# ConvFFN of a two-layer trunk: rstd moved from the FFN's input to its outputs, and the second group of columns computed in Strassen's block products

## The chip, the cores and the metric

One core of a Trainium2 chip runs the whole program. The metric is the device time of one execution in microseconds (us). TensorE is called PE here, VectorE DVE, ScalarE ACT, GpSimd POOL, and SyncE's DMA queue SP. PEld is PE's weight load, which runs beside its matmuls.

## The reference

The program computes a decoder trunk of two layers for 512 tokens of width 1024, in float32. Each layer is a pre-norm mixer and a pre-norm gated ConvFFN with residuals. What bears on this change:

```
def rms_norm(x, g):
    y = x32 * lax.rsqrt(jnp.mean(x32 * x32, axis=-1, keepdims=True) + EPS)
    return y.astype(x.dtype) * g

def gated_conv_ffn(x, w_gate, w_up, conv_w, conv_b, w_down):
    g = jnp.einsum('bsd,df->bsf', x, w_gate)
    g = causal_dwconv3(g, conv_w) + conv_b
    up = jnp.einsum('bsd,df->bsf', x, w_up)
    return jnp.einsum('bsf,fd->bsd', jax.nn.silu(g) * up, w_down)

h = h + gated_conv_ffn(rms_norm(h, norm_ffn[layer]), ...)
```

D_FF is 2816, that is 22 tiles of 128 columns. The factor rsqrt(mean) (called rstd, or r) belongs to a token, so it commutes with every product over the width: it may stand on the input of the two up-projections or on their outputs. The gate needs it ahead of its convolution over tokens; the up branch enters linearly, so its factor may stand anywhere up to the output of the down-projection.

## The kernel before

**Layout.** h is held as 8 tiles of 128 channels x 512 tokens. Every float32 operand of a matmul is split into two parts, hi (rounded by ACT) and lo (the rest, by DVE's subtraction or, in `summed`, L136, by an ACT copy of -x to which a DMA issued on POOL adds x). A product of two such operands is three matmuls (`mm3`, L152): hi·hi, hi·lo, lo·hi.

**The FFN.** It works through gate and up columns in groups of two tiles each (f, f+1), f = 0, 2, ..., 20, and after every second group adds the down-projection of the last four tiles to the residual (`PARTS`, L516; the first part projects two tiles only, so groups 0 and 2 run ahead of it). Layer 0 projects onto h with channels on the partitions (`project`, L286), layer 1 onto y with tokens on the partitions (`down` and `done`, L1106 and L1145).

- Group 0 (`direct`, L592) multiplies in the plain way: 4 column tiles x 8 channel tiles x 3 matmuls, each of 512 tokens. Its input is not normalized yet: hg holds gain·h. The norm's sums of squares are finished beside it, `rstd_cols` and `rstd_spread` (L222, L212) make r, and `evacuate` (L607) multiplies the gate by r on DVE (L615) and, after silu, the product's other factor by r on POOL (L618).
- Meanwhile `normalize` (L626) forms h·gain·r for all 8 channel tiles on DVE, splits it anew into hg (which group 0 is still reading), and makes the block sums t23 and t41 that Strassen's products need, split into halves too: by DVE for the first two pairs of channel tiles, by POOL's DMAs for the other two.
- Group 2 also runs `direct`, on the normalized hg, two column tiles at a time.
- Groups 4 to 20 run `both` (L681), Strassen's seven block products for gate and for up: 14 products of 4 x 3 matmuls, each of 256 tokens. The weights are first combined on DVE (s12, s34: L698 to L707) and split; `after` (L727) gathers products from PSUM into a padded row (gate) or into `kept` (up). After the products "g 4" and "g 3" the gate rows go through the convolution (`conv`, L561: one ACT scaling, two DVE operations) and silu. L750 to L755 multiply by the up part and split the result into the activations a_hi (ACT) and a_lo (DVE, L262).

**What sets the order.** The code is written in the order of priority, but each engine's queue is laid down ahead of time by the framework's planner, which takes the first instruction in this order whose inputs and buffers it reckons to be ready. So a matmul of a later product can be put ahead of one that would have to wait. On the chip each queue then runs in its fixed order. `inorder` pins single instructions to the written order, `behind` (L84) puts one behind another. Buffers bound it further: 7 PSUM banks for products, 6 weight units (whi, wlo), 4 activations, 3 tiles of the tag "sum" (x, t, s12, s34), 3 padded rows. The input weights arrive on SP's queue, whatever POOL adds to arrives on POOL's.

Of the kernel before, what the change touches and what calls it, by code (L numbers as in the profile page):

```python
# [32 lines left out]
def tile_trunk(ctx: ExitStack, tc: tile.TileContext, x, norm_mix, norm_ffn, final_norm,  # L33
# [102 lines left out]
    def summed(raw, a, b, name):  # L136

        hi = wp.tile([P, a, b], F32R, tag="whi", bufs=6, name=f"whi_{name}")
        lo = wp.tile([P, a, b], F32R, tag="wlo", bufs=6, name=f"wlo_{name}")
        first = nc.scalar.activation(lo, raw, AF.Copy, scale=-1.0)  # L140
        nc.gpsimd.dma_start(lo, raw, accum_op=ALU.add)  # L141
        behind(nc.scalar.activation(hi, raw, AF.Copy), first)
        return hi, lo
# [42 lines left out]
    def hg_k(k):  # L186
        return hg[k][0], hg[k][1]
# [358 lines left out]
    class Ffn:  # L546
# [7 lines left out]

        def __init__(self, layer, prm, norm, ap, sums):
# [3 lines left out]
            self.added = {"g": None, "u": None}  # L559

# [17 lines left out]
        def pair_weights(self, f, order, by_dma=""):  # L578

            ch = {}  # L580
            for key, half in order:
                name = f"{key}{self.layer}_{f}_{half}"
                raw = wp.tile([P, 4, 2 * P], F32, tag="raw", bufs=4, name=f"raw_{name}")
                w = (w_ffn_gate if key == "g" else w_ffn_up)[self.layer][:, f * P : (f + 2) * P]
# [4 lines left out]
                ch[key, half] = (summed if key in by_dma else parts)(raw, 4, 2 * P, name)  # L589
            return ch  # L590

        def direct(self, f, normed, sets, ch, before=lambda i, j: None):  # L592
# [3 lines left out]
            for js in sets:  # L596
                for i, k in enumerate(PAIRS):
                    for j in js:
                        before(i, j)
                        hi, lo = ch["gu"[j // 2], i // 4]  # L600
                        c = slice((j % 2) * P, (j % 2 + 1) * P)
                        if j not in banks:
                            banks[j] = mm_bank(f"gu{layer}_{f}_{j}")
                        mm3(banks[j], (hi[:, i % 4, c], lo[:, i % 4, c]), hg_k(k),
                            i == 0, i == NK - 1)

            def evacuate():  # L607
                r = self.r
                gates = []
                for j in range(2):  # L610
                    t = padded_tile()
                    if normed:
                        nc.scalar.copy(t[:, 2:], banks[j])
                    else:
                        nc.vector.tensor_tensor(t[:, 2:], banks[j], r, ALU.mult)  # L615
                    s = self.silu(self.conv(t, f + j), f + j)
                    if not normed:
                        nc.gpsimd.tensor_tensor(s, s, r, ALU.mult)  # L618
                    gates.append(s)
                for j, s in enumerate(gates):  # L620
                    nc.vector.tensor_tensor(s, banks[2 + j], s, ALU.mult)
                    self.act(f + j, s)
# [3 lines left out]
        def normalize(self, kp):  # L626

            n, r = f"{self.layer}_{kp}", self.r
            x = self.ap.tile([P, 2, S], F32, tag="sum", bufs=3, name=f"x{n}")
            for i, k in enumerate((kp, kp + NP)):  # L630
                nc.vector.scalar_tensor_tensor(x[:, i, :], h[k], self.prm("ffn", k), r,
                                               op0=ALU.mult, op1=ALU.mult)

            def halves(dst, src):
                nc.scalar.activation(dst[0], src, AF.Copy)
                nc.vector.tensor_tensor(dst[1], src, dst[0].bitcast(F32), ALU.subtract)

            halves(hg[kp], x[:, 0, :])
            halves(hg[kp + NP], x[:, 1, :])
            b11, b12 = x[:, 0, :HALF], x[:, 0, HALF:]  # L640
            b21, b22 = x[:, 1, :HALF], x[:, 1, HALF:]
# [546 lines left out]
```

## Time and profile before

| what | value |
|---|---|
| median of 3 runs | 994.29 us (994.14 to 994.36) |
| the profiled execution's own time | 994.15 us |
| its span, first to last instruction | 992.4 us |
| DVE busy | 728.5 us (73%) |
| ACT busy | 536.3 us (54%) |
| POOL busy | 105.3 us (11%) |
| bytes moved by DMA | 125.07 MB, mean 126 GB/s |

The profile is of one execution. A line of the timeline gives start, duration, engine, the code's line, the operation, output <- inputs, partitions x elements, and in brackets the idle time of that engine just before it with what ended it. A line of the windows gives, for a stretch from:to in us, its length and each engine's busy time with the number of instructions. A line of the groups gives the number of instructions after x, then busy time in all and the mean duration in ns. DVE's and ACT's durations overlap by some hundredths at their ends, so what an instruction costs its engine is the distance from one start to the next. The span is 1.75 us shorter than the execution's own time.

### The profile page before, as it was taken

To read this page: it belongs to the slowest core of one execution; us is meant where nothing else is said; L and a number is where in the kernel's file an instruction comes from. 1 tells how busy PE (TensorE), PEld (TensorE's weight loads), DVE (VectorE), ACT (ScalarE), POOL (GpSimd) and SP (SyncE) were. 2 spreads that over 40 slices of the span, in tenths; PEclk is the share of its full clock that TensorE was granted. 3 is DMA by queue.
4 is the path that set the end of the run, shared out by engine and by line. 5 is a ranking of instruction groups with operands and counts; after the bars stand their busy time and mean duration, and the time that the engine had idled before them with its cause. 6 is when DMAs were issued, how large, how long until landed. Compare 5 with 4: busy or idle time off the path is not lost.

```text
span 992.4 us, 14934 instructions
## 1 busy us (share of the span) xinstructions
PE 982.9 (99%) x5905; PEld 875.6 (88%) x5905; DVE 728.5 (73%) x1104; ACT 536.3 (54%) x806; POOL 105.3 (11%) x121
## 2 busy tenths in 40 slices
PE   9999999999999999999999999999999999999997
PEld 6788888898999989999888988888989899898996
DVE  6897458967785877858988665399668768687676
ACT  5623346744653746537668634675546366363664
POOL 2141031200000000000300001211000010000100
PEclk9999999999999999999999999999999999999999
DMA  7442225544553645536423513435546456464542
GB/s 246 133 146 85 86 88 131 121 148 118 133 147 97 181 121 132 148 98 180 136 87 93 182 54 97 105 91 130 143 101 159 124 125 173 94 163 126 123 112 85
DMA packets 83073, 125.07 MB, mean 126 GB/s; under 512 B 4308, under 2 KB 56252, under 8 KB 83004
## 3 DMA queue, kind: packets, MB, share of 16 engines
q1 hardware_dynamic: 74028, 98.24, 31.4%
q0 software_dynamic: 7056, 23.60, 13.3%
q10 hardware_dynamic: 1920, 2.30, 0.7%
q8 instruction: 46, 0.75, 0.3%
q14 instruction: 23, 0.19, 0.1%
HBM read 98.42 MB, written 2.10 MB: 101 GB/s over the span
## 4 chain that ended last, share of the span: by engine, by line
PE 94%; issue 1%; DVE 1%; DMA 1%; ACT 0%; DVEq 0%; POOLq 0%; ACTq 0%
PE d L154 4%; PE d L153 4%; PE d L155 4%; PE dn L153 4%; PE dn L154 4%; PE dn L155 4%; PE gu L153 3%; PE gu L154 3%; PE gu L155 3%; PE v L153 1%; PE oo L155 1%; PE oo L153 1%; PE v L155 1%; PE oe L155 1%; PE oe L154 1%; PE v L154 1%
## 5 line engine op out<-in xcount | busy, mean ns | idle before, releaser
L153 PE MATMUL dn<-whi_dn,a_hi 128*128 128x512 f32 (+1 forms) x180 | 69.4, 386 | 0.0
L154 PE MATMUL dn<-wlo_dn,a_hi 128*128 128x512 f32 (+1 forms) x180 | 69.3, 385 | 0.0
L154 PE MATMUL d<-a_lo,whi_d 128*128 128x512 f32 x176 | 68.7, 390 | 0.0
L155 PE MATMUL d<-a_hi,wlo_d 128*128 128x512 f32 x176 | 68.5, 389 | 0.0
L155 PE MATMUL dn<-whi_dn,a_lo 128*128 128x512 f32 (+1 forms) x180 | 67.9, 385 | 0.0
L153 PE MATMUL d<-a_hi,whi_d 128*128 128x512 f32 x176 | 66.9, 390 | 0.0
L566 DVE SCALAR_TENSOR_TENSOR c<-rows,prm,c 128x512 f32<-128x512 f32 x88 | 66.4, 766 | 0.0
L141 POOL DMA_DIRECT2D wlo_g<-raw_g x22 | 19.1, 867 | 373.9 <-ACT wlo_g L140 257.9
L1109 DVE TENSOR_TENSOR y<-dn,y 128x512 f32<-128x512 f32 (+1 forms) x49 | 32.5, 674 | 23.3 <-PE dn L155 23.0
L140 ACT ACTIVATE wlo_g<-raw_g 128x1024 fp32r<-128x1024 f32 x22 | 23.2, 1056 | 42.4 <-PE dn L154 42.4
L572 ACT ACTIVATE s<-c,prm 128x512 f32<-128x512 f32 x44 | 31.7, 720 | 20.5 <-DVE c L566 20.4
L679 DVE TENSOR_TENSOR wlo_s34u<-s34u,whi_s34u 128x1024 fp32r<-128x1024 f32 x18 | 22.0, 1225 | 27.9 <-ACT whi_s34u L678 27.9
L155 PEld LDWEIGHTS dn<-whi_dn,a_lo 128*128 128x128 f32 x180 | 33.8, 188 | 7.3 <-DVE a_lo L262 0.2
L678 ACT ACTIVATE whi_s12u<-s12u 128x1024 fp32r<-128x1024 f32 x18 | 18.9, 1051 | 39.3 <-PE d L154 33.7
L153 PEld LDWEIGHTS dn<-whi_dn,a_hi 128*128 128x128 f32 x180 | 33.8, 188 | 7.0 <-ACT a_hi L260 0.2
L154 PEld LDWEIGHTS dn<-wlo_dn,a_hi 128*128 128x128 f32 x180 | 33.8, 188 | 6.4
L154 PEld LDWEIGHTS d<-a_lo,whi_d 128*128 128x128 f32 x176 | 33.1, 188 | 7.3 <-DVE a_lo L262 0.2
L305 DVE TENSOR_TENSOR h<-d,h 128x512 f32<-128x512 f32 x48 | 32.5, 683 | 9.2 <-PE d L155 9.2
L153 PEld LDWEIGHTS d<-a_hi,whi_d 128*128 128x128 f32 x176 | 32.8, 188 | 7.0
L155 PEld LDWEIGHTS d<-a_hi,wlo_d 128*128 128x128 f32 x176 | 33.0, 188 | 6.7
L260 ACT ACTIVATE a_hi<-s 128x512 fp32r<-128x512 f32 x44 | 27.6, 628 | 16.1 <-DVE s L751 7.4
L149 DVE TENSOR_TENSOR wlo_dn<-raw_dn,whi_dn 128x1024 fp32r<-128x1024 f32 x22 | 26.8, 1220 | 11.6 <-ACT whi_dn L148 11.6
(1274 smaller groups left out, 3469.1 us busy)
## 6 DMA issues: line engine op xcount, KB each, us to landing
raw_g<-in_w_ffn_gate_dram SPq DMA_DIRECT2D x36, 512.0 KB, 4.6
raw_u<-in_w_ffn_up_dram SPq DMA_DIRECT2D x36, 512.0 KB, 4.7
wlo_g<-raw_g POOLq DMA_DIRECT2D x22, 512.0 KB, 4.7
raw_d<-in_w_ffn_down_dram SPq DMA_DIRECT2D x22, 512.0 KB, 4.0
raw_dn<-in_w_ffn_down_dram SPq DMA_DIRECT2D x22, 512.0 KB, 4.0
wlo_u<-raw_u POOLq DMA_DIRECT2D x19, 512.0 KB, 4.6
raw_oe<-in_w_out_even_dram SPq DMA_DIRECT2D x8, 512.0 KB, 3.6
raw_g<-in_w_ffn_gate_dram SPq DMA_DIRECT2D x16, 256.0 KB, 2.9
```

The source lines that it names most:

```text
L140: first = nc.scalar.activation(lo, raw, AF.Copy, scale=-1.0)
L141: nc.gpsimd.dma_start(lo, raw, accum_op=ALU.add)
L149: behind(nc.vector.tensor_tensor(lo, raw, hi.bitcast(F32), ALU.subtract), after[0])
L153: nc.tensor.matmul(ps, lhs[0], rhs[0], start=start, stop=False)
L154: nc.tensor.matmul(ps, lhs[0], rhs[1], start=False, stop=False)
L155: nc.tensor.matmul(ps, lhs[1], rhs[0], start=False, stop=stop)
L260: nc.scalar.activation(hi, src, AF.Copy, scale=scale)
L305: nc.vector.tensor_tensor(h[k], ps, h[k], ALU.add)
L566: nc.vector.scalar_tensor_tensor(c, t[:, i : S + i], prm("cf", i * NF + ft), c, op0=ALU.mult, op1=ALU.add)
L572: nc.scalar.activation(s, c, AF.Silu, bias=self.prm("bf", ft))
L679: nc.vector.tensor_tensor(lo, src, hi.bitcast(F32), ALU.subtract)
L1109: nc.vector.tensor_tensor(dst, ps, dst, ALU.add)
```

## The change

hg stays gain·h for the whole FFN, and r is applied behind the products. Group 2 runs `both` like the groups after it, and `direct` is left to group 0. In detail:

- `normalize` becomes `block_sums`: ACT scales one channel tile of a pair by the gain into the sum tile, DVE forms the four block sums from it and from h, and the sums are split as before, t41 ahead of t23. hg is not rewritten, and r is not needed for it.
- In `both`, each gate row is multiplied by r on DVE ahead of the convolution. In layer 0, whose down-projection has tokens along the free axis, DVE also multiplies the up branch's part by r: s[1] after its silu, and the first two blocks of kept. In layer 1 the factor of the up branch is applied where the down-projection's result is added to y: a column per token tile, as the scalar of one DVE operation in place of the plain addition. For that the column form of r is kept in `cols`.
- In `direct`, the multiplication by r after silu moves from POOL to DVE in layer 0 and goes away in layer 1.
- `summed` gets a hook: in `both` the split of s12 is written between the ACT copy that precedes POOL's DMA and the ACT copy of hi, where it stood ahead of both.

```
-    def summed(raw, a, b, name):
+    def summed(raw, a, b, name, between=lambda: None):
...
         first = nc.scalar.activation(lo, raw, AF.Copy, scale=-1.0)
         nc.gpsimd.dma_start(lo, raw, accum_op=ALU.add)
+        between()
         behind(nc.scalar.activation(hi, raw, AF.Copy), first)
...
+            self.cols = small[:, 3 * PAD : 3 * PAD + NT]
...
-                    if normed:
-                        nc.scalar.copy(t[:, 2:], banks[j])
-                    else:
-                        nc.vector.tensor_tensor(t[:, 2:], banks[j], r, ALU.mult)
-                    s = self.silu(self.conv(t, f + j), f + j)
-                    if not normed:
-                        nc.gpsimd.tensor_tensor(s, s, r, ALU.mult)
+                    nc.vector.tensor_tensor(t[:, 2:], banks[j], r, ALU.mult)
+                    s = self.silu(self.conv(t, j), j)
+                    if layer == 0:
+                        nc.vector.tensor_tensor(s, s, r, ALU.mult)
...
-        def normalize(self, kp):
+        def block_sums(self, kp):
+
+            n, g1, h1 = f"{self.layer}_{kp}", self.prm("ffn", kp + NP), h[kp + NP]
             t = self.ap.tile([P, 4, HALF], F32, tag="sum", bufs=3, name=f"t{n}")
-            nc.vector.tensor_tensor(t[:, 1, :], b22, b12, ALU.subtract)
+            b11, b12 = t[:, 2, :], t[:, 3, :]
+            nc.scalar.activation(t[:, 2:, :], h[kp].rearrange("p (a b) -> p a b", a=2), AF.Copy,
+                                 scale=self.prm("ffn", kp))
+            nc.vector.scalar_tensor_tensor(t[:, 1, :], h1[:, HALF:], g1, b12, op0=ALU.mult,
+                                           op1=ALU.subtract)
             nc.vector.tensor_tensor(t[:, 0, :], t[:, 1, :], b11, ALU.add)
-            nc.vector.tensor_tensor(t[:, 3, :], b12, b11, ALU.subtract)
-            nc.vector.tensor_tensor(t[:, 2, :], b21, t[:, 0, :], ALU.subtract)
+            nc.vector.tensor_tensor(b12, b12, b11, ALU.subtract)
+            nc.vector.scalar_tensor_tensor(b11, h1[:, :HALF], g1, t[:, 0, :], op0=ALU.mult,
+                                           op1=ALU.subtract)
...
-                self.halves(*w, s12)
+
+                def split_s12():
+                    self.halves(*w, s12)
+
+                hi, lo = summed(*raws[key, 1], between=split_s12)
...
-                hi, lo = summed(*raws[key, 1])
...
-                if (key, product) == ("g", 4):
-                    s[1] = self.silu(self.conv(pads[1], f + 1), f + 1)
-                elif (key, product) == ("g", 3):
-                    s[0] = self.silu(self.conv(pads[0], f), f)
+                if (key, product) in (("g", 4), ("g", 3)):
+                    j = product == 4
+                    row = pads[j][:, 2:]
+                    nc.vector.tensor_tensor(row, row, self.r, ALU.mult)
+                    s[j] = self.silu(self.conv(pads[j], f + j), f + j)
+                    if j and layer == 0:
+                        nc.vector.tensor_tensor(s[1], s[1], self.r, ALU.mult)
...
+            if layer == 0:
+                nc.vector.tensor_tensor(kept[:, :2, :], kept[:, :2, :],
+                                        self.r.rearrange("p (a b) -> p a b", a=2), ALU.mult)
...
-                        self.norm.rstd_cols(inorder)
+                        nc.vector.tensor_copy(self.cols, self.norm.rstd_cols(inorder))
...
-                self.ch = self.pair_weights(2, [("g", 0), ("g", 1), ("u", 0), ("u", 1)], "g")
                 for kp in range(NP):
-                    self.normalize(kp)
+                    self.block_sums(kp)
                 rest()
-            elif f == 2:
-                self.direct(2, True, ((0, 1), (2, 3)), self.ch)()
             else:
                 self.both(f)
...
-                    nc.vector.tensor_tensor(dst, ps, dst, ALU.add)
+                    nc.vector.scalar_tensor_tensor(dst, ps, ffn.cols[:, t : t + 1], dst,
+                                                   op0=ALU.mult, op1=ALU.add)
```

More of the change, by code (lines that the diff above doesn't have):

```diff
@@ L588, in pair_weights, with direct @@
                                       w[:, h_, 2 * half : 2 * half + 2])
-                ch[key, half] = (summed if key in by_dma else parts)(raw, 4, 2 * P, name)
+                ch[key, half] = parts(raw, 4, 2 * P, name)
             return ch
-        def direct(self, f, normed, sets, ch, before=lambda i, j: None):
+        def direct(self, ch, before):
             layer = self.layer
             banks = {}
[L596 to L605, printed above, removed]
+            for i, k in enumerate(PAIRS):
+                for j in range(4):
+                    before(i, j)
+                    hi, lo = ch["gu"[j // 2], i // 4]
+                    c = slice((j % 2) * P, (j % 2 + 1) * P)
+                    if j not in banks:
+                        banks[j] = mm_bank(f"gu{layer}_{j}")
+                    mm3(banks[j], (hi[:, i % 4, c], lo[:, i % 4, c]), hg_k(k),
+                        i == 0, i == NK - 1)
             def evacuate():
@@ L621, in evacuate @@
                     nc.vector.tensor_tensor(s, banks[2 + j], s, ALU.mult)
-                    self.act(f + j, s)
+                    self.act(j, s)
             return evacuate
-        def normalize(self, kp):
[L628 to L641, printed above, removed]
-            t = self.ap.tile([P, 4, HALF], F32, tag="sum", bufs=3, name=f"t{n}")
-            nc.vector.tensor_tensor(t[:, 1, :], b22, b12, ALU.subtract)
+        def block_sums(self, kp):
+            n, g1, h1 = f"{self.layer}_{kp}", self.prm("ffn", kp + NP), h[kp + NP]
+            t = self.ap.tile([P, 4, HALF], F32, tag="sum", bufs=3, name=f"t{n}")
+            b11, b12 = t[:, 2, :], t[:, 3, :]
[3 more added lines that the diff above has]
+                                           op1=ALU.subtract)
             nc.vector.tensor_tensor(t[:, 0, :], t[:, 1, :], b11, ALU.add)
-            nc.vector.tensor_tensor(t[:, 3, :], b12, b11, ALU.subtract)
-            nc.vector.tensor_tensor(t[:, 2, :], b21, t[:, 0, :], ALU.subtract)
+            nc.vector.tensor_tensor(b12, b12, b11, ALU.subtract)
+            nc.vector.scalar_tensor_tensor(b11, h1[:, :HALF], g1, t[:, 0, :], op0=ALU.mult,
+                                           op1=ALU.subtract)
             self.t23[kp] = self.sums(kp)
```

14 lines of the change are left out of this document (7 added, 7 removed).

## The prediction

> **What bounds the kernel now.** First the page's head, then the waits of PE.
>
> ```profile
> span 992.4 us, 14934 instructions
> PE 982.9 (99%) x5905; PEld 875.6 (88%) x5905; DVE 728.5 (73%) x1104; ACT 536.3 (54%) x806; POOL 105.3 (11%) x121
> PE clock L62 <- DVE idle L57: 1.3, 1, 1.3
> PE u_20b L535 <- DMA wlo_u<-raw_u: 0.8, 1, 0.8
> PE z L415 <- ACT hgh L392: 0.4, 1, 0.4
> ```
>
> PE is busy for all but 9.5 us, and only three waits of it are listed, 2.5 us together. So time can come off in two ways only: PE's own work gets less, or the 0.8 us wait goes. And time is added wherever PE is made to wait. Next, windows over seven stretches: the plain group 0 (147.50 on), the plain group 2, the small projection, Strassen's group 4; then group 8, its projection and group 10, which show one period of the steady course.
>
> ```profile
> 147.50:169.32 21.82, 21.82 (x104) 18.09 (x102) 16.45 (x32) 12.81 (x20) 2.58 (x3) 1.00 0.59 145
> 169.32:191.08 21.76, 21.76 (x98) 18.02 (x96) 20.54 (x34) 16.38 (x27) 6.46 (x6) 1.00 0.47 97
> 191.08:202.10 11.02, 11.02 (x51) 9.15 (x50) 11.02 (x17) 6.12 (x7) 0.87 (x1) 1.00 0.53 143
> 202.10:222.26 20.16, 20.16 (x170) 20.16 (x169) 11.47 (x17) 11.33 (x18) 0.86 (x1) 1.00 0.48 138
> 264.25:284.40 20.15, 20.15 (x169) 20.12 (x169) 15.41 (x24) 14.35 (x24) 0.85 (x1) 1.00 0.64 177
> 284.40:306.20 21.80, 21.80 (x98) 17.90 (x97) 18.00 (x29) 7.92 (x10) 0.85 (x1) 1.00 0.50 138
> 306.20:326.40 20.20, 20.20 (x170) 20.20 (x169) 12.60 (x20) 11.30 (x18) 1.70 (x2) 1.00 0.38 92
> ```
>
> The columns after the length are PE, PEld, DVE, ACT, POOL, granted clock (full everywhere). PE is full in each. A plain group takes 21.76 us, a Strassen group 20.16. DVE is at 46.0 of the 62.15 us of a period (15.41 + 18.00 + 12.60), but full or nearly so from 169 to 202.
>
> **The change, part by part.** *PE's work.* A plain group is 4 x 8 x 3 = 96 matmuls of 512 tokens, 21.76 / 96 = 0.2267 us each; a Strassen group 14 x 4 x 3 = 168 of 256 tokens, 20.16 / 168 = 0.120 each. The columns streamed fall by an eighth, which would be 2.72 us; but PEld is full in Strassen's windows (20.16 of 20.16) and not in the plain ones (18.02 of 21.76), so part of it goes to 72 more weight loads. The rows give 1.60 us per layer, 3.20 in both. The Trainium skill (TensorE: Matmul & The Clock Gate, Back-to-back issue gap) speaks against the change: it gives sustained spacings of about 81 ns at 128 columns and 131 at 512. On a straight line between, an estimate, that is 98 at 256, and Strassen's group would be 168 x 0.098 - 96 x 0.131 = 3.9 us longer, 7.8 in both layers. This trace disagrees, at 120 and 227 ns. By the same section's formula for a lone stream (N / 2.4 + 2.5 ns) the gain would be 2.4 us per layer.
>
> *Entry into the group.*
>
> ```profile
> 264.25 1.44 PE g_8a L535 x12
> 271.44 1.51 PE u_8a L535 x12
> ```
>
> Where a Strassen group runs straight behind another group, one of its 14 products takes 1.51 for 1.44. Group 2 will stand behind group 0: +0.07 per layer, +0.14.
>
> *The one wait.*
>
> ```profile
> 944.23 1.05 ACT L678 ACTIVATE whi_s12u<-s12u 128x1024 fp32r<-128x1024 f32 x1
> 947.53 1.04 ACT L140 ACTIVATE wlo_u<-raw_u 128x1024 fp32r<-128x1024 f32 x1
> 948.88 5.94 DMA wlo_u<-raw_u
> ```
>
> PE waited 0.81 us for this addition by DMA. The ACT copy ahead of it started 3.3 us after s12's split; written ahead of that split it can take its place, 0.95 us or more earlier, which is more than the wait. I take -0.81; the ends are 0 (a buffer comes free no sooner) and a loss, since s12's split now runs 0.95 us later, to which the second rival below gives a price.
>
> *What a new DVE operation costs.* In one stretch without idle:
>
> ```profile
> 283.30 0.74 DVE L566 SCALAR_TENSOR_TENSOR c<-rows,prm,c 128x512 f32<-128x512 f32 x1
> 283.96 1.22 DVE L149 TENSOR_TENSOR wlo_d<-raw_d,whi_d 128x1024 fp32r<-128x1024 f32 x1
> 285.10 0.74 DVE L566 SCALAR_TENSOR_TENSOR c<-rows,prm,c 128x512 f32<-128x512 f32 x1
> 286.75 0.42 DVE L750 TENSOR_TENSOR s<-kept,s 128x256 f32<-128x256 f32 x1
> 287.09 0.41 DVE L751 TENSOR_TENSOR s<-u_8a,s 128x256 f32<-128x256 f32 x1
> 290.43 0.68 DVE L698 TENSOR_TENSOR s12g<-raw_g,raw_g 128x512 f32<-128x512 f32 x1
> 291.03 0.68 DVE L705 TENSOR_TENSOR s34g<-raw_g 128x512 f32<-128x512 f32 x1
> ```
>
> From start to start: 0.60 us for a two-input operation of 512, 0.34 of 256, 1.14 of 1024, and 0.66 for one with a scalar column. So the multiplications by r cost 4 x 0.60 = 2.4 us per group in layer 0 and 2 x 0.60 = 1.2 in layer 1, in ten groups each. A period of layer 0 rises from 46.0 to 50.8 of 62.15 us: DVE does not become the bound on the whole. A block sum with a gain column (256 wide) has no row; it lies between 0.34 and 0.66, eight of them per layer, so at most 2.6 us, hidden where DVE idles.
>
> *The first stage.*
>
> ```profile
> 154.44 1.41 DVE L631 SCALAR_TENSOR_TENSOR x<-h,prm,rstd_f 128x512 f32<-128x512 f32 x2 [2.05 <-ACT rstd_f L219]
> L631 DVE SCALAR_TENSOR_TENSOR x<-h,prm,rstd_f 128x512 f32<-128x512 f32 x16 | 11.7, 743 | 4.1 <-ACT rstd_f L219 4.1
> L636 DVE TENSOR_TENSOR hgl<-x,hgh 128x512 fp32r<-128x512 f32 x16 | 10.5, 680 | 0.0
> ```
>
> Per layer DVE loses 8 normalizations and 8 splits: 8 x 0.66 + 8 x 0.60 = 10.1 us. Group 2's plain form goes: two weight splits (2.3), four convolution steps (2.6), two products and two splits (2.4), 7.3 us. Its Strassen form comes: weights 10 x 0.60 + 4 x 1.14 = 10.6, gathering 6 x 0.34, convolution 2.6, products and splits 2 x 0.34 + 3 x 0.60, together 17.7, and 2.4 or 1.2 for r. Layer 0 also takes over POOL's two multiplications, 1.2. Net: -10.1 - 7.3 + 17.7 + 2.4 + 1.2 = +3.9 in layer 0, -17.4 + 17.7 + 1.2 = +1.5 in layer 1. From 147.50 to 222.26 DVE idles 5.4 + 1.2 + 0 + 8.7 = 15.3 us, and the first 5.4, which now wait for r until 154.44, become usable, since the block sums need only h. ACT is at 16.4 of 21.8 at most, and loses the 8 hg copies. So I cost this stage at nothing; if the cover is gone it costs at most the 3.9. What is late next is then s12u's split: as the fifth weight unit of group 2 it finds a buffer only when group 0's last matmul gives one back, and PE asks for it four products (5.8 us) later, against 1.05 + 1.22 us for its two halves.
>
> *The ends of the parts.* Here the new operations stand in the chain itself: rows, convolution, silu, product, split.
>
> ```profile
> 284.31 0.40 PE L153 MATMUL d<-a_hi,whi_d 128*128 128x512 f32 x1
> 289.56 0.86 PE L153 MATMUL d<-a_hi,whi_d 128*128 128x512 f32 x3
> 288.74 0.63 ACT L260 ACTIVATE a_hi<-s 128x512 fp32r<-128x512 f32 x1 [0.51 <-DVE s L754]
> 289.83 0.68 DVE L262 TENSOR_TENSOR a_lo<-s,a_hi 128x512 fp32r<-128x512 f32 x1
> ```
>
> PE runs the part's first two tiles over four banks from 284.31 to 289.56 and then takes the new activation, whose hi half was done at 289.37: 0.2 us to spare. With up to 2.4 us more of DVE work the halves come up to 2.4 us later. PE then needs other work: of 7 banks the projection holds 4, and three more outputs of the first two tiles are 3 x 2 x 3 x 0.2267 = 4.1 us, their weights being split by 285.1 (the row of 283.96 above is the last of them). 4.1 covers 2.4, and DVE's splits of the next group's weights, which stood in between, can be put off as well. I take 0; the ends are 0 and 2.4 x 5 + 1.2 x 5 = 18.0.
>
> *The tail.*
>
> ```profile
> L394 DVE SCALAR_TENSOR_TENSOR hgl<-xt_ps,prmmix,hgh x8: 739/750/752, 7.0 to 27.7; 128x512 fp32r<-128x512 f32 x8
> L305 DVE TENSOR_TENSOR h<-d,h 128x512 f32<-128x512 f32 x48 | 32.5, 683 | 9.2 <-PE d L155 9.2
> ```
>
> Scaling while adding from PSUM costs 0.750 for 0.683. Only the last piece of 256 is on the path: +0.03.
>
> **Sum**, on the execution's own 994.15: -3.20 - 0.81 + 0.14 + 0.03 = 990.31. The median of the runs lies 0.14 above it: **990.5**.
>
> **The rivals.** *A: given back where a second group follows the first one of its pair* (8, 12, 16, 20).
>
> ```profile
> 268.33 1.22 DVE L679 TENSOR_TENSOR wlo_s12u<-s12u,whi_s12u 128x1024 fp32r<-128x1024 f32 x1
> 269.85 0.40 PE L535 MATMUL u_8e<-t,whi_s12u 128*128 128x256 f32 x2
> 261.59 0.85 POOL L141 DMA_DIRECT2D wlo_g<-raw_g  x1 [15.25 <-PE g_6e L535]
> ```
>
> The split of s12u ends 0.3 us before PE takes it, and the 2.4 us of layer 0 fall ahead of it on DVE's queue. PE can draw one product forward (g 2, 1.44 us, its weights having been sent for at 261.59). Left are 2.4 - 0.3 - 1.44 = 0.66 us, four times: +2.6, **993.1**. In layer 1 1.2 is covered. For it speaks that DVE is full there; against it that s34g's split, which ran ahead of s12u's, can change places with it. Chance 0.22.
>
> *B, slower: the ends of the parts are not covered.* Place: the ten first matmuls on a pair's second activations. Price: 18.0 in full, **1008.5**; a third of it 996.5. It decides from the point at which the chain is later than what PE still has to do, that is, if the planner cannot give the projection a fifth bank, or reckons the chain sooner than the chip runs it and so leaves PE's queue in the old order. For it: 0.2 us to spare today. Against it: in no such place does PE wait now, so the planner's reckoning holds. Chance 0.17.
>
> *C: the change does not lessen PE's work.* Strassen's form breaks even at 21.76 / 168 = 0.1295 us a matmul; there only the wait goes, 994.15 - 0.81 + 0.14 + 0.03 + 0.14 = **993.7**; at 0.140 it adds 168 x 0.0105 x 2 = 3.5, 997.2. The rows speak against it: the Strassen windows above all give 0.120. Chance 0.03. The Trainium skill's section named above is what makes this case.
>
> **How the numbers follow.** Forecast 0.58, own range 989.8 to 992. What a measurement here can tell from no change is about 0.2%, 2 us: faster is below 992.3, slower above 996.3. Faster: 0.58 and 0.04 of A = 0.62. Same: 0.18 of A, 0.02 each of B and C = 0.22. Slower: 0.15 of B, 0.01 of C = 0.16. The range runs from 989.8 (PE has no other wait to lose) to 997.0, which takes in A and a third of B.
>
> **What would show it.** Group 2 at 20.2 us on PE in both layers; no wait of PE for wlo_u; a first stage without a wait; in the projections of layer 0, more than eight products of first tiles ahead of the first new activation, and no wait there; DVE near 50.8 us a period. It is wrong if PE's list of waits names a_hi, a_lo, wlo_s12u or t.

## The result, and the profile after

The change makes the kernel **slower**: a median of 1008.98 us (1007.37 to 1009.86, 4 runs) against 994.21 (994.08 to 994.36, 4 runs), ratio 1.0146, interval 1.0133 to 1.0159. Forecast was 990.5. First the head of the page after, and the waits of PE (in all, times, longest).

```profile
span 1008.2 us, 15288 instructions
PE 986.8 (98%) x6049; PEld 882.2 (88%) x6049; DVE 769.6 (76%) x1174; ACT 543.8 (54%) x816; POOL 101.0 (10%) x117
PE v L154 <- ACT v L941: 2.7, 1, 2.7
PE u_2e L536 <- DVE wlo_s12u L671: 2.7, 2, 2.1
PE ssc_f L227 <- POOL ssq_f L210: 1.9, 1, 1.9
PE ssr_f L217 <- DVE rc_f1c L251: 0.9, 1, 0.9
PE u_16e L536 <- ACT whi_s12u L670: 0.8, 1, 0.8
PE u_12e L536 <- ACT whi_s12u L670: 0.8, 1, 0.8
PE u_20e L536 <- ACT whi_s12u L670: 0.8, 1, 0.8
PE u_8e L536 <- ACT whi_s12u L670: 0.7, 1, 0.7
```

The wait for wlo_u is gone, and in these rows nine others have come, 11.3 us in all. PE's busy time should have fallen by 3.2 us and has risen by 3.9, so something also makes matmuls longer. The windows of groups 0, 2, 4, then 8, its projection and 10, each from its first matmul on (columns PE, PEld, DVE, ACT, POOL, then the clock, the DMA engines' share and GB/s):

```profile
146.45:173.35 26.90, 24.99 (x109) 20.30 (x108) 20.45 (x41) 16.65 (x26) 7.90 (x7) 0.94 0.45 98
173.35:194.76 21.41, 20.66 (x170) 20.25 (x168) 18.49 (x29) 15.89 (x25) 0.85 (x1) 1.00 0.47 123
205.67:226.13 20.46, 20.41 (x169) 20.20 (x168) 15.29 (x20) 12.49 (x19) 0.85 (x1) 1.00 0.55 161
268.21:289.43 21.22, 20.53 (x172) 20.30 (x171) 17.98 (x29) 13.56 (x22) 0.86 (x1) 1.00 0.48 129
289.43:311.33 21.90, 21.90 (x98) 17.94 (x97) 19.97 (x33) 9.18 (x12) 0.86 (x1) 1.00 0.50 136
311.33:331.49 20.16, 20.16 (x170) 20.15 (x169) 12.82 (x19) 11.65 (x18) 1.72 (x2) 1.00 0.54 134
```

Group 0 of before is to be set beside the first row from its own first matmul on. The window of 147.50 in the prediction begins 1.37 us behind that.

```profile
146.13:169.32 23.19, 23.19 (x110) 19.22 (x108) 17.14 (x33) 14.18 (x22) 3.95 (x4) 1.00 0.56 137
```

DVE is at 17.98 + 19.97 + 12.82 = 50.8 us a period, as forecast, and the projection at 21.90 is covered but for 0.1. The time is lost in groups 0, 2 and 8, and group 0's clock stands at 0.94. The next table is worked out from PE's timeline of each kernel: from the first matmul of a stage to the first of the next, in us, like stages added up. Its last five columns are runs 3, 5, 6, 8 and 9 below.

```
stage                     before   after  no r mult  v order  first stage  sums ahead  all three
groups 0 + 2, layer 0      44.95   48.31    47.89     46.80      44.03       46.28       43.98
group 4, layer 0           20.15   20.46    20.15     20.52      20.83       20.14       20.82
groups 8,12,16,20, l. 0    80.94   84.85    80.97     84.85      84.86       81.49       81.42
mixer 1, from v to u       65.16   69.69    65.16     65.09      68.30       66.41       65.09
groups 0 + 2, layer 1      48.13   50.79    51.55     50.80      49.05       50.48       48.89
group 4, layer 1           20.15   20.46    20.15     20.47      20.85       20.46       20.86
groups 8,12,16,20, l. 1    82.05   80.88    80.97     80.89      81.16       80.64       80.64
eleven projections        218.36  219.32   218.38    219.39     219.30      219.41      219.31
```

Between before and after, the rows add up to 14.9 of the 15.8 us that the span has grown. The first stages (groups 0 and 2) have taken 6.0 in place of giving 3.2, the second groups of layer 0 3.9, mixer 1 4.5. I follow each to its place. Against the forecast the first stages lose 9.2 us in four pieces: group 0 takes 26.90 for 23.19 in layer 0 and 27.51 for 26.37 in layer 1, group 2 takes 21.41 and 23.28 for 20.15.

**Group 0, layer 0.** DVE, POOL and PE, and the window behind the wait:

```profile
146.46 1.44 DVE L671 TENSOR_TENSOR wlo_a<-raw_g,whi_a 128x512 fp32r<-128x512 f32 x1 [0.29 <-ACT whi_a L670]
147.82 0.68 DVE L306 TENSOR_TENSOR h<-oe,h 128x512 f32<-128x512 f32 x1
149.91 2.64 POOL L210 TENSOR_TENSOR ssq_f<-ssq_f,sq_f 128x512 f32<-128x512 f32 x1 [2.57 <-DVE t L635]
152.60 1.05 PE L227 MATMUL ssc_f<-small,ssq_f 128*128 128x1 f32 x8 [1.91 <-POOL ssq_f L210]
154.86:158.27 3.41, 3.41 (x10) 0.50 0.51 96
```

In the kernel before, in the same views:

```profile
146.33 0.69 DVE L305 TENSOR_TENSOR h<-oe,h 128x512 f32<-128x512 f32 x1 [0.49 <-PE oe L155]
148.77 1.29 POOL L209 TENSOR_TENSOR ssq_f<-ssq_f,sq_f 128x512 f32<-128x512 f32 x1 [0.79 <-ACT sq_f L208]
```

The block sums and the a11 splits of group 2 no longer need r. So the planner put them ahead of the last piece of the norm's chain: the last addition to h runs 1.5 us later (0.3 of it from the program's start), and POOL's last sum of squares, now beside DVE operations with two inputs, takes 2.64 for 1.29. PE's pinned matmul of the sums waits 1.91 us. From 2.3 us later on PE's clock stands at one half for 3.41 us (the last row is of PE alone). That costs 1.56: run 5 has the same wait without such a stretch, and its group 0 takes 25.34.

**The second groups of layer 0**, DVE and ACT of after:

```profile
272.50 0.68 DVE L752 TENSOR_TENSOR kept<-kept,rstd_f 128x512 f32<-128x512 f32 x1
273.10 0.68 DVE L692 TENSOR_TENSOR s12u<-s12u,raw_u 128x512 f32<-128x512 f32 x1
273.82 1.06 ACT L670 ACTIVATE whi_s12u<-s12u 128x1024 fp32r<-128x1024 f32 x1 [0.57 <-DVE s12u L692]
```

and of before:

```profile
261.75 0.68 DVE L700 TENSOR_TENSOR s12u<-s12u,raw_u 128x512 f32<-128x512 f32 x1
```

The second sum of s12u stood ahead of group 6's chain of convolutions, 2.3 us before group 8 began. Now it stands behind that chain and behind all four multiplications by r, 4.9 us after group 8's start at 268.21.

**Mixer 1.** DVE and PE of after, the window of PE's wait, and the issue of the transfers:

```profile
518.32 1.22 DVE L899 TENSOR_TENSOR raw_u<-raw_u,raw_u 128x1024 f32<-128x1024 f32 x1 [4.78 <-DMA raw_u<-in_w_in_odd_dram]
520.59 1.41 DVE L851 SCALAR_TENSOR_TENSOR nx<-h,prm,rstd_m 128x512 f32<-128x512 f32 x2
529.20 0.50 PE L154 MATMUL v<-whi_v,hgh 128*128 128x512 f32 x1 [2.69 <-ACT v L941]
529.00:535.00 6.00, 5.80 (x18) 4.62 (x19) 6.00 (x11) 6.00 (x14) 0.00 (x0) 0.72 0.00 0
510.19 2.64 SPq L130 DMA_DIRECT2D raw_u<-in_w_in_odd_dram  x3
```

and the same difference of weight blocks, and its transfers, in before:

```profile
497.03 4.34 SPq L130 DMA_DIRECT2D raw_u<-in_w_in_odd_dram  x3
505.87 1.23 DVE L901 TENSOR_TENSOR raw_u<-raw_u,raw_u 128x1024 f32<-128x1024 f32 x1 [2.61 <-DMA raw_u<-in_w_in_odd_dram]
```

This instruction heads DVE's queue in both kernels and waits there for a transfer; the normalization of mixer 1 stands behind it. The transfers wait for buffers that DVE's splits of v's weights give back; these splits come later, and the first transfer is issued 9.0 us into the stage (501.19) where it was issued after 4.1 (492.92). r itself is ready 13.8 us into the stage in both kernels, so it is not what the normalization waits for. DVE stands idle for 4.78 us instead of 2.61, and PE waits 2.69 for the Gelu, followed again by half clock.

### The profile page after: what moved, and what is told of

Same layout as the page of the kernel before. It is cut to its first block, busy times and chain, and to the rows that moved or that the text cites. A ratio compares the mean times of both kernels' runs of the same rounds, so it can differ in the third digit from the quotient of the medians.

```text
span 1008.2 us, 15288 instructions
## 1 busy us (share of the span) xinstructions
PE 986.8 (98%) x6049; PEld 882.2 (88%) x6049; DVE 769.6 (76%) x1174; ACT 543.8 (54%) x816; POOL 101.0 (10%) x117
## 5 line engine op out<-in xcount | busy, mean ns | idle before, releaser
L1107 DVE SCALAR_TENSOR_TENSOR y<-dn,small,y 128x512 f32<-128x512 f32 (+1 forms) x49 | 35.4, 734 | 18.4 <-PE dn L156 18.2
L141 POOL DMA_DIRECT2D wlo_u<-raw_u x21 | 18.1, 860 | 286.2 <-ACT wlo_u L140 168.5
L143 ACT ACTIVATE whi_g<-raw_g 128x1024 fp32r<-128x1024 f32 x20 | 21.1, 1055 | 41.7 <-PE dn L156 41.7
L568 ACT ACTIVATE c<-rows,prm 128x512 f32<-128x512 f32 x44 | 31.2, 716 | 19.5 <-DVE rows L744 18.6
L671 DVE TENSOR_TENSOR wlo_s34u<-s34u,whi_s34u 128x1024 fp32r<-128x1024 f32 x20 | 24.5, 1224 | 19.6 <-ACT whi_s34u L670 19.6
L670 ACT ACTIVATE whi_s12u<-s12u 128x1024 fp32r<-128x1024 f32 x20 | 21.0, 1052 | 31.5 <-PE d L155 22.0
```

The lines of the kernel that those rows point to most:

```text
L568: nc.scalar.activation(c, t[:, 0:S], AF.Copy, scale=prm("cf", ft))
L671: nc.vector.tensor_tensor(lo, src, hi.bitcast(F32), ALU.subtract)
L1107: nc.vector.scalar_tensor_tensor(dst, ps, ffn.cols[:, t : t + 1], dst, op0=ALU.mult, op1=ALU.add)
```

## The experiments

Two theories were set against each other. The **queue theory**: each wait comes from work that was put ahead of what PE needs next; the added work itself costs little. The **load theory**: the multiplications by r make DVE late. Diffs are against the kernel after unless another is named, medians stand against 994.3 to 994.6 us of the kernel before on the same chip, and a ratio is to that one.

**1. s12's split where it stood before**, in every group.

```
...
-                hi, lo = summed(*raws[key, 1], between=split_s12)
+                self.halves(*w, s12)
...
                 nc.vector.tensor_tensor(s34[:, 1], r1[:, :, :P], s12[:, 1], ALU.subtract)
+                hi, lo = summed(*raws[key, 1])
```

> The changed kernel with one part undone: the split of s12 is written where it stood, ahead of the ACT copy for POOL's DMA. Queue theory (each wait of PE comes from work that was put ahead of what PE needs, the added DVE work itself costs little): the four second groups of layer 0, which each wait 0.7 to 0.8 us for ACT's half of s12u, go from 21.21 back to 20.23 us, 4 us off; the 0.8 us wait for wlo_u in layer 1's last group may come back; 1005 to 1006. Load theory (the multiplications by r make DVE late, wherever the rest stands): no change, 1009.

1006.02, ratio 1.0117 (1.0102 to 1.0132). The waits of the second groups change their name:

```profile
PE u_20b L536 <- DMA wlo_u<-raw_u: 1.3, 2, 1.0
PE u_8b L536 <- DMA wlo_u<-raw_u: 1.2, 2, 0.7
```

In the second groups the order of split and copy is thus not the cause: whichever comes second is late (84.25 us for 84.85 in layer 0). In layer 1, where after has no such wait, the old order waits for wlo_u and loses 3.2. In group 2 it is another matter:

```profile
669.22:690.84 21.62, 20.58 (x169) 20.24 (x168) 18.51 (x29) 15.73 (x25) 0.86 (x1) 1.00 0.60 169
```

It takes 21.62 for 23.28 in layer 1, where group 0 is unchanged (27.50), and 20.15 for 21.41 in layer 0. So the change's own move of s12's split, made for the one wait, costs group 2 up to 2.9 us. Neither theory had this: that the median lies at the edge of the queue theory's 1005 to 1006 is luck, for the 4 us it wanted in the second groups did not come.

**2. The norm's chain first**: the block sums and the a11 splits of group 2 are put behind the last square on ACT and behind the copy of r on DVE, and so, on DVE, are group 2's weight sums.

```
-            nc.scalar.activation(t[:, 2:, :], h[kp].rearrange(...), AF.Copy, ...)
+            behind(nc.scalar.activation(t[:, 2:, :], h[kp].rearrange(...), AF.Copy, ...), self.norm.last)
-            nc.vector.scalar_tensor_tensor(t[:, 1, :], h1[:, HALF:], g1, b12, ...)
+            behind(nc.vector.scalar_tensor_tensor(t[:, 1, :], h1[:, HALF:], g1, b12, ...), self.copied)
...
+                        self.added = {"g": self.copied, "u": self.copied}
```

> The changed kernel with group 2's preparation (block sums, weight splits and sums) put behind the norm: ACT's behind the last square, DVE's behind the last small operation of rstd. Queue theory: in layer 0 group 0 goes from 26.9 back to about 23.2 us, with no wait of PE for ssq and no stretch at half clock behind it, in layer 1 from 27.5 to 26.4; about 1004. The waits of group 2 for wlo_s12u stay or grow by up to 2 us. Load theory: the same work done later is late later, no gain, 1009 or more.

1005.56, 1.0111 (1.0096 to 1.0126). Group 0 is back at 23.20 and 26.37 us, and its wait is gone: that loss, 3.7 and 1.1 us with the 1.6 of the clock, was order alone. Group 2, prepared later, takes 22.38 in layer 0 (21.41 in after) and 22.62 in layer 1 (23.28), and group 4 of layer 0 loses 0.8.

**3. No multiplications by r in the Strassen groups**, which leaves that part of the computation out; group 0 keeps its own.

```
-                    nc.vector.tensor_tensor(row, row, self.r, ALU.mult)
-                    if j and layer == 0:
-                        nc.vector.tensor_tensor(s[1], s[1], self.r, ALU.mult)
...
-            if layer == 0:
-                nc.vector.tensor_tensor(kept[:, :2, :], kept[:, :2, :], ...)
```

> The changed kernel without the multiplications by r in the Strassen groups: rows, s[1] and kept are left unscaled, so the output is not the reference's. 2.4 us of DVE work per group of layer 0 and 1.2 of layer 1 are gone, 36 us in all. Load theory: nearly all of the loss goes, 990 to 993. Queue theory: group 0 stays at 26.9 us, the second groups of layer 0 keep most of their 0.8 us waits; 1005 to 1009.

1000.10, 1.0056 (1.0038 to 1.0074). The table's third column: second groups, mixer 1 and projections are back to before, the first stages are not. The first of mixer 1's transfers is issued 4.1 us into the stage again. So the multiplications are what makes DVE late in the first three places, about 9 us, and those of the Strassen groups have little part in the first stages (0.4 us in layer 0, none in layer 1).

**4. Strassen alone**: the kernel before, its input normalized as it was, with group 2 in Strassen's form.

```
-                self.ch = self.pair_weights(2, [("g", 0), ("g", 1), ("u", 0), ("u", 1)], "g")
-            elif f == 2:
-                self.direct(2, True, ((0, 1), (2, 3)), self.ch)()
```

> The other part alone: the kernel before, its input normalized as before, with group 2 in Strassen's products. PE's work falls by 3.2 us in both theories. Queue theory: the norm's chain is not crowded, since the block sums need r; group 0 stays at 23.2 us; 991 to 993, if s12u's split in group 2 is not late. Load theory: DVE, which was full from 169 to 202 us with 7.3 us of plain work in place of 17.7, is late by 3 to 8 us per layer; 994 to 1005.

1025.27, 1.0309 (1.0292 to 1.0326). Group 2 takes 37.16 and 35.78 us:

```profile
PE g_2e L535 <- ACT whi_s12g L678: 12.4, 2, 6.4
PE g_2e L535 <- DVE wlo_s12g L679: 4.1, 2, 3.0
```

In this order normalization and the weight sums don't both fit beside group 0, and from the midst of the long waits on PE's clock stands at one half for 13.65 us in each layer. Strassen's group 2 alone is thus far slower than both halves of the change together; another order of it was not run.

**5. One instruction of mixer 1**: the block difference behind the second of the normalization's four pairs of channel tiles (`normed[1]`), not behind its last instruction, as the expectation below has it.

```
-                    nc.vector.tensor_tensor(b12, b12, b11, ALU.subtract)
+                    behind(nc.vector.tensor_tensor(b12, b12, b11, ALU.subtract), first)
...
-            u0.rest()
+            u0.rest(normed[1])
```

> The kernel after, with one instruction of mixer 1 moved: the difference of two weight blocks that DVE makes for the u projection (L899 of the kernel after) is held behind the normalization's last instruction, so that DVE does not stand 4.8 us at the head of its queue for the transfer raw_u while r has long been ready. Queue theory: the stage from v to the end of u, 69.69 us in the kernel after, goes back to about 65.2-66, so 1008.98 becomes about 1004.5-1005.5, and the wait of v for the Gelu goes. Load theory: what is late is DVE's and POOL's sums of the last outputs themselves; then r comes as late as before, v waits as long, and the time stays within 1 us of 1009.

1005.26, 1.0106 (1.0091 to 1.0121), and the stage from v to u:

```profile
514.16 1.42 DVE L851 SCALAR_TENSOR_TENSOR nx<-h,prm,rstd_m 128x512 f32<-128x512 f32 x2
499.71:564.80 65.09, 65.09 (x373) 57.48 (x372) 54.05 (x80) 50.50 (x83) 8.08 (x6) 1.00 0.35 105
```

The normalization starts 14.5 us into the stage, where it started 19.4 in after, and the whole 4.6 are back, 1.6 of them by the clock. The first transfer is issued as late as in after, 9.0 us in. With run 3 both conditions are shown: the multiplications make the transfer late, and the queue order makes PE pay for it.

**6. The first stage in another order**: as run 2, and group 0's evacuation is written between group 2's s12u and s34u splits.

```
+                if key == "u" and midway is not None:
+                    midway()
                 w = self.unit(f"s34{key}_{n}")
```

> The kernel after, with the first stage in another order: group 2's block sums and a11 splits stand behind the last squares of the norm and behind the copy of r, as in the run before with that edit, and the plain group's evacuation (its convolutions and silu) is written between group 2's s12u split and its s34u split, no longer ahead of all its splits. Queue theory: group 0 goes to 23.2 (layer 0) and 26.4 (layer 1), group 2 to about 20.2 in both, so 3.7+1.2+1.1+3.1, about 9 us less than the kernel after: near 1000; the second groups (21.2) and v stay. Load theory: DVE has too much in these 45 us whatever the order; group 2 stays at 21.4-23 and something else, the convolutions' banks or s34u, is waited for: 1004-1006.

1003.93, 1.0097 (1.0082 to 1.0112). Group 0 is right again. Group 2 comes to 20.83 and 22.68 and not to 20.2, and group 4 loses 0.4 in each layer. The 5 us won are half of what the queue theory wanted.

**7. r on the outputs alone**, group 2 plain on the unnormalized input.

```
+                self.ch = self.pair_weights([("g", 0), ("g", 1), ("u", 0), ("u", 1)], 2, "g")
...
+            elif f == 2:
+                self.direct(self.ch, lambda i, j: None, 2, ((0, 1), (2, 3)))()
```

> One part of the change alone: the FFN input is not normalized and r is applied on the outputs, but group 2 stays plain (its weights' split as in the kernel before, its products on the unnormalized input). Load theory: the second groups of layer 0 stay at 21.2 and v at 69.7, because the multiplications by r are still there; group 2 takes 21.8: about 1005-1009. Queue theory: without the block sums ahead of the norm's chain group 0 takes 23.2-24.4, and group 2 21.8, which is 44.9-46.2 for the two against 48.3 in the kernel after; the second groups as in the load theory, v less if its lateness comes from group 2's splits: 1000-1005.

1002.76, 1.0081 (1.0066 to 1.0096). The first stages take 44.93 and 48.13, exactly as before; the second groups of layer 0 stay at 21.2 each and the stage of v at 69.07. So moving r costs about 8 us by itself, none of it in groups 0 and 2, and their loss comes only with Strassen's preparation.

**8. The sums of the second groups one step earlier** on DVE, ahead of the evacuation of product g 4 of the group before.

```
+                if (key, product) == ("g", 4) and f % 4 == 2 and f > 2:
+                    self.make_ahead(f + 2)
                 after(key, product, self.multiply(banks[key], f"{key}{n}", product,
```

> The kernel after, with the weight sums s12g, s34g and s12u of the second groups (8, 12, 16, 20) written one step earlier on DVE: ahead of the evacuation of the product g4 of the group before them, which now holds the multiplications by r. Queue theory: the second groups of layer 0 go from 21.21 to 20.23, 4 us less: about 1005, and u_8e, u_12e, u_16e and u_20e no longer wait for whi_s12u. Load theory: the same work stands on DVE in the same period, so the wait moves to another tile of these groups or to the groups between them and less than 1.5 us is won.

1001.78, 1.0082 (1.0065 to 1.0099). DVE and ACT:

```profile
263.00 0.68 DVE L679 TENSOR_TENSOR s12u<-s12u,raw_u 128x512 f32<-128x512 f32 x1
264.45 1.06 ACT L670 ACTIVATE whi_s12u<-s12u 128x1024 fp32r<-128x1024 f32 x1 [0.43 <-PE u_6a L536]
```

The sum now lies 2.8 us ahead of group 8's start (265.76), where it lay 4.9 behind it; its waits are gone, and 3.4 of 3.9 us come back there, with DVE's work unchanged. So the four multiplications fit, if what PE needs stands ahead of them. Not expected: mixer 1 gains 3.3 as well, its first transfer being issued 6.2 us into the stage for 9.0.

**9. All three orders together** (6, 5 and 8).

> The three edits that each won something, together: norm's chain first with the plain group's evacuation in the midst of group 2's preparation; the block difference of mixer 1 behind the normalization; the second groups' sums one step earlier. If the gains add up by stages (queue theory): group 0 at 23.2 and 26.4, group 2 at 20.8 and 22.7, second groups of layer 0 at 20.3, v at 65.1, and 0.8 won in layer 1's last group: 1008.98 - 3.7 - 0.6 - 1.1 - 0.6 - 3.7 - 4.6, about 994.5, no different from the kernel before. Load theory: work pushed out of one place makes another late, the gains overlap: 997-1000.

996.14 (995.62 to 996.37, 11 runs), 1.0016 (1.0008 to 1.0025). Of the versions that do the whole computation none is faster (run 10 is level with it), and it still lies about 1.7 us above the kernel before. The spans differ by 1008.2 - 993.9 = 14.3, as expected by stages; the medians by 12.8, since the profiled execution of after was 0.9 above its median (1009.86) and that of run 9 was 0.5 below its own (995.62). The table's last column shows what is left: mixer 1 nothing, second groups 0.5, projections 1.0, group 4 1.4, and group 2 0.6 and 2.4 above its 20.15.

**10 to 14, what holds group 2.** In run 9 the third weight sum of layer 1's group 2, s34g, waits for a sum buffer that a transfer still reads:

```profile
658.35 0.69 DVE L682 TENSOR_TENSOR s34g<-raw_g 128x512 f32<-128x512 f32 x1 [2.46 <-DMA t<-t]
```

The **buffer theory**: group 2 is held by such buffers. Run 10 lets the transfers make the low halves of the first two of the four pairs (`if kp >= 2` for `if kp < 2`); 11 has s12's split ahead in group 2 alone (as 1, for f == 2); 12 does both; 13 has four sum buffers for three, and two silu buffers for three to make room; 14 is 11 with 13.

> The combined kernel, with the block sums' splits shared out otherwise: the first two of the four have their low half from the accumulating transfer, the last two from DVE (it was the other way round). In the trace s34g and s12u of group 2 wait for buffers that those transfers still read. Queue theory: with the transfers on the first two tiles these buffers come free earlier, group 2 goes from 20.8 and 22.7 to 20.2-21, 1 to 2.5 us less than the combined kernel. Load theory: DVE's amount of work is unchanged, group 2 stays within 0.5.

> The combined kernel, with s12's split ahead of the negated copy of raw in group 2 alone (in the kernel before it stood there in every group). Queue theory: u_2e no longer waits for wlo_s12u; what comes later is the lo of raw_u by its transfer, for u_2b: group 2 near 20.2 in layer 0 and 21.6 in layer 1, as in the run with that order in all groups: 1.5 us less than the combined kernel. Load theory: no gain, the wait changes its name.

> Both of the last two edits on the combined kernel. Queue theory: group 2 at 20.2 in both layers, all waits but 0.5 us gone, and then what is left of the change is its forecast gain: 994.5 - 3.2 - 0.8 + 0.5 for the rest, about 991-992, faster than before. Load theory: DVE holds it at 994 or above.

> The combined kernel, with four buffers for the block and weight sums in place of three (and two for the gates in place of three, to make room). In the combined kernel s12u of group 2 is made 0.8 us after DVE is free, when the last block sum's transfer lets its buffer go. Queue theory: group 2 goes from 20.8 and 22.5 to 20.2-21, the time from 996.1 to 994 or a little less. Load theory: DVE is full from the end of the norm to the first product of group 4, a buffer changes nothing: within 0.5 of 996.1.

> The same with s12's split ahead of the negated copy in group 2. Queue theory: as the run before, or better by what u_2e still waits: 993-995. Load theory: the wait moves to group 4 as it did with three buffers, 996-998.

None wins. In the order of the runs: 996.25 (1.0019, 1.0010 to 1.0028), 997.91 (1.0036, 1.0024 to 1.0049), 999.74 (1.0049, 1.0035 to 1.0062), 999.17 (1.0045, 1.0031 to 1.0060) and 997.57 (1.0031, 1.0019 to 1.0042). Every edit moves PE's wait. In 11 group 2 of layer 1 gains 1.1 us and group 4 behind it loses 1.0; in layer 0 both lose. In 13 the wait stands in layer 0 (PE, and the window behind it):

```profile
176.16 0.39 PE L536 MATMUL g_2a<-t23h,whi_s12g 128*128 128x256 f32 x1 [1.98 <-ACT rows L753]
177.20:180.40 3.20, 3.20 (x17) 3.20 (x16) 3.20 (x5) 3.17 (x5) 0.00 (x0) 0.50 0.65 129
```

PE now waits for ACT to empty a bank, and in the 3.2 us behind that, at half clock, DVE and ACT are both full. Run 9 has DVE at 20.68 of group 2's 20.78 us:

```profile
169.18:189.96 20.78, 20.41 (x169) 20.20 (x168) 20.68 (x33) 15.57 (x24) 0.86 (x1) 1.00 0.68 192
660.96:683.48 22.52, 20.92 (x169) 20.31 (x168) 19.80 (x30) 16.27 (x25) 1.72 (x2) 1.00 0.68 184
```

So in layer 0 DVE has hardly room left for another order, though that none would help is not shown (in run 1 group 2 took 20.15 there, behind a slower group 0). The buffer theory found no support: with four buffers group 2 took 23.88 and 22.09 us, 1.6 of the first by the clock, though run 13 also has a silu buffer less. In layer 1 DVE has 2.7 us free, and which of its waits would have to go is not settled.

**15. Run 9 without the multiplications by r** in the Strassen groups, as in run 3.

> The combined kernel without the multiplications by r in the Strassen groups (the plain group keeps its own): their gates and up products stay unscaled, so this part of the computation is left out. It tells what of the remainder is DVE's load. Load theory: the ends of the parts go from 21.9 back to 21.82, about 1.2 us over eleven of them, group 4 to 20.15 twice (1.4), group 2 hardly, since its own multiplications come after it: about 993.5. Queue theory: the ends of the parts alone, 995.

993.98, 0.9993 (0.9984 to 1.0003). Projections 218.45, group 4 20.15 and 20.47, second groups 80.98; group 2 stays at 20.78 and 22.72. Of run 9's time 2.2 us is the multiplications' load; group 2's delay is not.

**16. One multiplication on GpSimd** (run 9, `nc.gpsimd` for kept).

> The combined kernel, with the multiplication of the kept up products by r in layer 0 on GpSimd, so that DVE has three such multiplications a group in place of four. Load theory: part ends of layer 0 come back by about 0.1 each and group 4 by some tenths: 995.5. Queue theory: GpSimd's product takes longer than DVE's 0.69 and the last gate of the group waits for it; as there are 40 us until that gate is used no stage of PE changes: within 0.5 of 996.1.

1006.39, 1.0119 (1.0104 to 1.0133), against both theories. POOL, and PE's waits:

```profile
289.81 2.26 POOL L783 TENSOR_TENSOR kept<-kept,rstd_f 128x512 f32<-128x512 f32 x1 [20.33 <-DVE kept L758]
PE d L154 <- ACT a_hi L261: 3.8, 5, 0.9
PE u_8a L536 <- ACT kept L753: 1.1, 1, 1.1
```

GpSimd takes 1.61 to 2.26 us for DVE's 0.68: kept, which has one buffer, comes free too late for the next group, and the activation too late for the projection. Here the prediction's rival B does happen: 22.8 to 23.0 us a projection.

Taken together: by medians the change lost 14.8 us, order alone (run 9) gives 12.8 of them back, and 2.2 more go with the multiplications' load (run 15). The forecast 990.5 is not reached even then; group 2, 0.6 us too long in layer 0 and 2.6 in layer 1, stays open.

## Why the prediction was wrong

- *PE's work and entry*: right. Where nothing waits, a Strassen group takes 20.15 to 20.2.
- *The one wait*: right in its place. Layer 1's last group went from 21.33 to 20.24, 1.1 for the 0.8 forecast. The loss by which the prediction bounded this term, s12's split running later, came too: up to 2.9 us in group 2 (run 1).
- *The first stage*, costed at nothing: **this step failed**, by 3.36 + 1.60 in layer 0 and 2.66 + 1.60 in layer 1, 9.2 us, of which 1.6 are the clock's. Its bound, 3.9 if the cover goes, was an amount of DVE's work. DVE's busy time from group 0 to group 4 rose by 5.1 and 3.6 us for the 3.9 and 1.5 counted, but runs 1, 2 and 6, which change only the order, win 5.4, 4.5 and 6.0 of the 9.2 us back there. The idle time ahead of r was not free to fill: it lay in front of the norm's own chain, and what filled it came ahead of that chain (run 2: 3.7 us in group 0 of layer 0 and 1.1 in layer 1). s12u's split, named there as next late, was late indeed, because the change's new place for it let group 0's two rows and four convolutions, 4 us, go in front of it, and the 5.8 us to spare did not cover that. This is layer 1 of after:

```profile
675.90 1.28 DVE L615 TENSOR_TENSOR rows<-gu,rstd_f 128x512 f32<-128x512 f32 x2
677.38 2.74 DVE L570 SCALAR_TENSOR_TENSOR c<-rows,prm,c 128x512 f32<-128x512 f32 x4 [0.20 <-ACT c L568]
680.03 1.22 DVE L671 TENSOR_TENSOR wlo_s12u<-s12u,whi_s12u 128x1024 fp32r<-128x1024 f32 x1
681.30 0.39 PE L536 MATMUL u_2e<-t,wlo_s12u 128*128 128x256 f32 x1 [2.06 <-DVE wlo_s12u L671]
```

- *Rival A*, given a chance of 0.22, was the right mechanism for the second groups. It cost 1.0 us a group for 0.66, because the second sum, not only the split, fell behind the chain.
- *The ends of the parts*: taken as 0, measured 0.96 over eleven; the planner did find other work, as argued. Rival B is not what made the kernel slower.
- *Mixer 1*, 4.5 us, is in no step: the prediction put it at nothing without a reason. The DVE instruction of before that waits 2.61 us for a transfer at the head of the queue was in the trace, with nothing of the change near it. I followed the late activations to the end of their own projection and no further.
- *The clock*: granted full in every window of before, and I took it so. In after two waits of PE are followed by half clock, about 1.6 us each.

## What to carry to other kernels

Work freed from a dependency does not go where the idle time is, but wherever the planner's order lets it; if that is ahead of the chain that PE waits for next, pin it behind. An added DVE operation that fits by the period's sum still costs if it stands ahead of the next group's operands: moving those sums 7.7 us forward gave back 3.4 of 3.9 us. And look for instructions that already wait for a transfer at the head of a queue: they cost nothing until something upstream comes later. Before a gain is credited to an edit, see whether a stretch at half clock came or went with it: here one is worth 1.6 us.

## What the runs showed of the hardware

Over after and the variants but run 4, the 22 waits of PE between 0.85 and 1.71 us past the program's first 10 us were not followed by a lower clock. Of 17 waits of 1.90 to 2.69 us, 9 were followed by one stretch of 3.41 us at 0.50, starting 0.2 to 2.3 us later, and 8 by none. It isn't the length that decides: the 1.91 us wait of group 0 had it in after and in run 3, and not in runs 5 and 8. It goes with how the wait falls on a grid. Within a run the stretches start whole multiples of 3.413 us apart (after: 154.86 and 530.33, 110 steps; run 12: 145; run 3: 152), and so does the one at each program's end, which gives the grid of the runs that have no other. On it every step that was followed by a stretch held at least 1.95 us in which PE stood idle or did only the eight one-column matmuls of a norm, and no other step held more than 1.81. In after group 0's wait put 1.16 us and these matmuls 0.92 into one step, 2.07 together; in run 5 the same wait was cut into 1.11 and 0.80, and the second step came to 1.72. In run 4, with waits of 6 us, one stretch began behind a step with 1.46. Such a stretch costs 1.6 us, so run 5's and run 8's gains hold 1.6 in group 0 that are not theirs.

The Trainium skill (TensorE: Matmul & The Clock Gate, What's actually happening) describes a free-running window of 3.4 us. The length of the stretches and the grid agree with that. Its condition of a whole idle window does not: 1.95 of 3.41 us were enough here.

In after one of POOL's 14 sums of squares for the FFN's norms took 2.64 us, amid DVE operations with two SBUF inputs; their median is 1.29. Two such DVE operations took longer beside a sum of squares: the split at 146.46, which started behind POOL's sum of 146.05, took 1.44 for 0.68 (POOL's own took 1.29), and a block sum at 151.35 took 1.48 for 0.47. The Trainium skill (SBUF — State Buffer, Who interferes with whom) says that a DVE instruction with two SBUF inputs and a GpSimd instruction that reads SBUF contend; the trace agrees.
